# Weighing values by whole fp32 products on the two column halves of TensorE

## The chip, the core and the metric

One core of one Trainium2 chip runs the program. TensorE (PE in the profile, PEld its weight loads) multiplies, VectorE (DVE) and ScalarE (ACT) do the elementwise work, GpSimd (POOL) small work, and SyncE (SP) issues most of the transfers. The metric is the device time of one execution in microseconds; the kernel before took 608.46 us (median of 3 runs, 608.0 to 609.45).

## The reference, cut to what matters

Two layers of an encoder on 256 tokens of width 1024, all in fp32. Each layer is an attention sublayer with 16 heads of width 64 in three groups, each head with its own 256 x 256 matrix of probabilities, and then a gated feed-forward sublayer of width 2816.

```python
def mixer_sublayer(x, n1, w_in_l, qg, kg, rpb_l, og, w_out_l, tables):
    h = rms_norm(x, n1)
    proj = h @ w_in_l
    ...
    out_a = neighbourhood_attention(qa, ka, heads(va, H_NA), ...)   # 4 heads
    out_d = dilated_window_attention(qd, kd, heads(vd, H_DIL), ...) # 6 heads
    out_c = gqa_block_attention(qc, kc, heads(vc, H_GKV))           # 6 heads, 2 sets of keys and values
    mix = jnp.concatenate([rms_norm(out_a, ...), rms_norm(out_d, ...), rms_norm(out_c, ...)], axis=-1)
    return x + mix @ w_out_l

def channel_sublayer(x, n2, w_gu, cw, cb, w_dn):
    g, u = jnp.split(rms_norm(x, n2) @ w_gu, 2, axis=-1)
    g = depthwise_conv_centred(g, cw, cb)
    return x + (jax.nn.gelu(g, approximate=False) * u) @ w_dn
```

What the change touches is, in every head, the last step: p = softmax(scores), then p times the head's values (256 x 256 by 256 x 64).

## The kernel before, in words

**Split parts.** The kernel gets fp32 accuracy out of products of the type fp32r: each operand is split into a large part (`hi`, the cast) and a little part (`lo`, what the cast leaves), and `mm3` (L708) makes one product of three: large by large, large by little, little by large. ACT makes the large parts and DVE the little ones, for the weights (`split`, L676, tiles `wp_hi` and `wp_lo`) as for the activations. The profile's names follow the buffers: `psw_w` and `psa_a` are the two pools of PSUM banks.

**Attention.** In each layer the projections run first as a "filler" on TensorE, between them and then between the output projections the steps of the heads are woven in (`Weave`, L764; the loop at L1298). A head's steps are `scores` (L1226: products of 64 rows, two heads side by side on the two row halves of TensorE, kept together in bursts by `nc.together()`), `softens` (softmax on DVE and ACT), `turn` (L1105) and `weigh` (L1121, called by L1261). `turn` transposes the probabilities with four TensorE transposes into one PSUM tile, which ACT copies as the large part (`act_ch`) and from which DVE makes the little part (`act_cl`). `weigh` multiplies values by the turned probabilities: for each of two blocks of 128 keys, three products of a 128 x 128 stationary operand and 256 moving columns. The stationary operand is a head's 64 columns of values beside 64 columns of zeros (`beside_zeros`, L1065; tiles `const_v`, whose zeros GpSimd writes at the start, L601), on the left for an even head and on the right for an odd one, so that both heads of a pair add into one PSUM tile of 128 rows. So a pair takes 12 products, and a layer has 8 pairs. `mixed` (L1130) reads the sum into the operands of the output projection.

**The order of the work** is not the program's order. `Plan` (L239) records all instructions first. `order` (L323) then simulates the engines with the costs of `cost` (L475) and takes, again and again, the instruction that could start first; among equals the lowest rank goes first. The rank is the instruction's number in the program, shifted by `later` and by the table `PLACES` (L229), which holds a shift for single instructions by number. The start of matmuls on PE is reckoned by `run_on_pe` (L385). The first 13 loads (`START`, L45: the input, the identity, gains and the first four chunks of weights, on SP's and ACT's queues) are given fixed landing times by their place in the program (`LANDS`, L52, used at L450), wherever the order puts them. Each engine then runs its instructions strictly in the order that comes out.

The kernel fills the first microseconds of PE with products of no use (`warmed`, L581; `const_warm`).

Of the kernel before, what the change touches and what calls it, by code (L numbers as in the profile page):

```python
# [36 lines left out]
UNIT = 2048  # L37
BANK = 512
NS2K = 5


RAWS, PARTS, AHEAD, CHUNK = 4, 2, 2, 512
# [182 lines left out]
def handover(a, b):  # L225
# [1 line left out]


PLACES = {  # L229
# [6 lines left out]
}  # L236


class Plan:  # L239
# [83 lines left out]
    def order(self):  # L323
# [60 lines left out]

        def run_on_pe(o, at):  # L385

            half = o.kind == "half"
            if pe is None:
                return at + 109, o.ns, half, False
            start, ns, was, open_ = pe  # L390
            if half and was:
                ld = max(start + 3, at)
                if open_:
                    return max(start + 4, ld + (0 if at <= start + 3 else 109)), o.ns, half, False
                return max(start + 113, ld + 109), o.ns, half, True
            if half or was:
                return max(start + ns + 92, at) + 108, o.ns, half, True
            return max(start + ns, max(start + 3, at) + (106 if o.kind == "turn" else 110)), o.ns, half, False

        done = []  # L400
        gone = [False] * len(ops)
# [1 line left out]
        while len(done) < len(ops):  # L403
# [71 lines left out]
def cost(engine, method, args, kw, ins):  # L475
# [42 lines left out]
def encoder_kernel(  # L518
# [70 lines left out]
    with nc.later(1000):  # L589
# [299 lines left out]
    for l in range(DEPTH):  # L889
# [161 lines left out]
                transposed(pairs(zs[t], first, n), both, t, f"{what}{group}{l}{t}")  # L1051
            return both

        def values(places, src, t):

            hi, lo = places
            r = rx[:, t : t + 1]
# [3 lines left out]
        def values_of(tiles, ps, c0, t, nh):  # L1061
            src = ps[:, c0 : c0 + nh * HD].rearrange("p (h d) -> p h d", d=HD)
            values([z[:, t, 1 : 2 * nh : 2] for z in tiles], src, t)

        def beside_zeros(tiles, h, odd):  # L1065

            i = 2 * h + 1 - odd
            return [z[:, :, i : i + 2].rearrange("p t m d -> p t (m d)") for z in tiles]


        class Head:
# [33 lines left out]
            def turn(self):  # L1105
                name = self.name
                tp = psw.tile([P, NT, S], F32, tag="w", name=f"tp_{name}")
                for kt in range(NT):
                    for t in range(NT):
                        nc.tensor.transpose(  # L1110
                            tp[:, kt, t * P : (t + 1) * P], self.p[:, t, kt * P : (kt + 1) * P], ident
                        )
                self.pT = [
                    act.tile([P, NT, S], F32R, tag=g, name=f"pT{g}_{name}", bufs=2) for g in ("ch", "cl")
                ]
                hi, lo = self.pT
# [4 lines left out]
            def weigh(self, op, first, last):  # L1121

                hi, lo = self.pT
                for kt in range(NT):
                    mm3(
                        op, self.v[0][:, kt], self.v[1][:, kt], hi[:, kt], lo[:, kt],
                        first and kt == 0, last and kt == NT - 1,
                    )

        def mixed(op, gi, i):  # L1130

# [113 lines left out]

        heads = []
        for h in range(H_DIL):
            heads.append(Head("d", h, h, [dil[:, t] for t in range(NT)], beside_zeros(vown, h, h % 2)))
        for h in range(H_GQ):
            kv = h // (H_GQ // H_GKV)  # L1250
            heads.append(Head("c", h, kv, None, beside_zeros(vkv, kv, h % 2)))
        for h in range(H_NA):
            heads.append(Head("a", h, h, na_bias(h), beside_zeros(vown, h, h % 2)))

        def values_a():
            for t in range(NT):
# [2 lines left out]
        groups = [(gi, h) for gi, n in enumerate((H_DIL, H_GQ, H_NA)) for h in range(n)]  # L1259

        def weigh(i):  # L1261
            gi, h = groups[i]
            if h % 2 == 0:
                hold["op"] = psw.tile([P, S], F32, tag="w", name=f"o_{l}{i}")
            heads[i].weigh(hold["op"], h % 2 == 0, h % 2 == 1)
            if h % 2 == 1:
                with nc.later(MIX_LATER):
                    mixed(hold["op"], gi, h // 2)

        prep_d("q", gq)  # L1270
        wv.until("dk")
# [26 lines left out]
        for i in range(len(heads) + 2):  # L1298
            for part in range(3):
                if (i, part) in hooks:  # L1300
                    with nc.later(PREP_LATER):
                        hooks[i, part]()
                if part == 0 and i < len(heads) and i % 2 == 0:
                    scores(i)
                elif part == 1 and 0 <= i - 1 < len(heads):
                    heads[i - 1].turn()
                elif part == 2 and 0 <= i - 2 < len(heads):
                    weigh(i - 2)
                    if i - 2 in (7, 12):
                        group_rstd((i - 2) // 12)  # L1310
        wv.fill(1e9)
        group_rstd(2)

# [238 lines left out]
```

## Time and profile before

| | before |
|---|---|
| median of 3 runs | 608.46 us |
| lowest, highest | 608.0, 609.45 us |
| span of the profiled execution, first to last instruction | 606.6 us |
| PE busy in it | 600.9 us (99%) |
| DVE busy | 484.9 us (80%) |
| ACT busy | 428.6 us (71%) |
| POOL busy | 80.9 us (13%) |

The span is what the trace shows of one execution; the profiled execution has no other time of its own in the data, and the median of the runs lies 1.8 us above its span. A line of the timeline gives the start in us from the start of the span, the length in us of one or several instructions merged, the engine, the operation with out<-in and shapes, and how many. The lengths of neighbouring matmuls overlap: what one costs in a row of them is the distance from start to start. All instructions carry line L472, the one place that emits them, so they are told apart by tile names. The notes on waits in brackets give the idle time before an instruction and what ended it.

### The profile page before, as it was taken

The numbers are of one execution on the slowest core, as the hardware profiler recorded it, in microseconds if no ns is written. First come the engines' busy times: TensorE is split into PE (matmuls) and PEld (weight loads), VectorE is DVE, ScalarE is ACT, GpSimd is POOL, SyncE is SP. The second block draws the span as 40 slices with busy tenths as digits, with TensorE's granted clock in tenths as the row PEclk, the third lists the DMA queues.
The fourth block names the chain that finished last, engine by engine and source line by source line (L and its number), as shares of the span: only waits on it lengthen the run. The fifth ranks groups of instructions, "written<-read, shape, count | busy, mean of one in ns | idle before, by whom it ended". The sixth has DMA issues, their size and how long they took to land.

```text
span 606.6 us, 9899 instructions
## 1 busy us (share of the span) xinstructions
PE 600.9 (99%) x3496; PEld 526.7 (87%) x3496; DVE 484.9 (80%) x995; ACT 428.6 (71%) x1065; POOL 80.9 (13%) x130
## 2 busy tenths in 40 slices
PE   8999999999999999999999999999999999999997
PEld 7999898888888888888899989888888888888886
DVE  4899897997788988887777898777977777777775
ACT  6889999686666767666688899676765555665661
POOL 2733030103400000000022214421000000000000
PEclk9999999999999999999999999999999999999999
DMA  8994303566598899988455726844465555555601
GB/s 280 296 294 140 105 36 107 195 202 228 185 224 297 278 342 322 318 304 290 153 147 162 248 70 243 291 163 139 142 205 209 174 175 206 184 166 207 199 9 69
DMA packets 85217, 121.44 MB, mean 200 GB/s; under 512 B 9880, under 2 KB 69880, under 8 KB 85168
## 3 DMA queue, kind: packets, MB, share of 16 engines
q1 hardware_dynamic: 82896, 112.17, 56.3%
q0 software_dynamic: 1728, 8.39, 3.9%
q8 instruction: 27, 0.44, 0.3%
q10 hardware_dynamic: 544, 0.26, 0.2%
q14 instruction: 22, 0.18, 0.1%
HBM read 110.93 MB, written 9.88 MB: 199 GB/s over the span
## 4 chain that ended last, share of the span: by engine, by line
PE 96%; ACT 2%; DVE 1%; POOL 0%; issue 0%; DVEq 0%; ACTq 0%; POOLq 0%
PE psw_w L472 53%; PE psa_a L472 43%; ACT act_s2k L472 1%; ACT wp_hi L472 0%; DVE act_z L472 0%; DVE wp_lo L472 0%; POOL small_rstd L472 0%; ACT act_z L472 0%; ACT act_hT L472 0%; DVE act_sw L472 0%; POOL small_ms L472 0%; DVE const_x L472 0%; DVE act_qo L472 0%; POOL const_warm L472 0%; DVEq L472 0%
## 5 line engine op out<-in xcount | busy, mean ns | idle before, releaser
L472 DVE TENSOR_TENSOR wp_lo<-wp_raw,wp_hi 128x512 fp32r<-128x512 f32 (+2 forms) x332 | 231.5, 731 | 59.1 <-ACT wp_hi L472 39.3
L472 ACT CAST wp_hi<-wp_raw 128x512 fp32r<-128x512 f32 (+2 forms) x332 | 203.0, 663 | 22.8 <-PE psw_w L472 10.2
L472 PE MATMUL psw_w<-act_hT,wp_hi 128*128 128x512 f32 x704 | 180.4, 393 | 0.0
L472 PEld LDWEIGHTS psw_w<-act_hT,wp_hi 128*128 128x128 f32 x704 | 127.8, 189 | 24.8 <-DVE act_hT L472 0.7
L472 PE MATMUL psa_a<-wp_hi,act_hT 128*128 128x384 f32 (+2 forms) x448 | 113.1, 333 | 0.7 <-ACT wp_hi L472 0.7
L472 PEld LDWEIGHTS psw_w<-act_hT,wp_lo 128*128 128x128 f32 x704 | 97.7, 190 | 6.8
L472 PE MATMUL psw_w<-act_hT,wp_lo 128*128 128x256 f32 x704 | 102.2, 282 | 0.0
L472 PEld LDWEIGHTS psa_a<-wp_hi,act_hT 128*128 128x128 f32 x448 | 78.3, 189 | 3.4 <-ACT wp_hi L472 0.9
L472 ACT COPY act_s2k<-psw_w 128x256 f32<-128x256 f32 x88 | 32.4, 373 | 62.2 <-PE psw_w L472 61.9
L472 PE MATMUL psa_a<-wp_lo,act_hT 128*128 128x384 f32 (+2 forms) x224 | 74.4, 334 | 0.1
L472 PE MATMUL psa_a<-wp_lo,act_ch 128*128 128x512 f32 (+1 forms) x176 | 68.9, 392 | 0.0
L472 PE MATMUL psa_a<-wp_hi,act_ch 128*128 128x512 f32 x176 | 68.8, 392 | 0.0
L472 PE MATMUL psa_a<-wp_hi,act_cl 128*128 128x512 f32 (+1 forms) x176 | 68.5, 393 | 0.0
L472 DVE TENSOR_TENSOR act_s2k<-psw_w,act_s2k 128x256 f32<-128x256 f32 x88 | 36.6, 421 | 14.5 <-ACT act_s2k L472 14.1
L472 PEld LDWEIGHTS psa_a<-wp_lo,act_hT 128*128 128x128 f32 x224 | 42.2, 189 | 2.4 <-DVE wp_lo L472 1.0
L472 PEld LDWEIGHTS psa_a<-wp_hi,act_cl 128*128 128x128 f32 x176 | 33.1, 188 | 7.5
L472 PEld LDWEIGHTS psa_a<-wp_hi,act_ch 128*128 128x128 f32 x176 | 33.2, 189 | 6.7
L472 PEld LDWEIGHTS psa_a<-wp_lo,act_ch 128*128 128x128 f32 x176 | 33.1, 188 | 6.7
L472 DVE SCALAR_TENSOR_TENSOR act_s2k<-act_s2k,act_cw,act_s2k 128x255 f32<-128x255 f32 x88 | 36.7, 477 | 1.4 <-ACT act_s2k L472 1.3
L472 ACT ACTIVATE act_s2k<-act_s2k 128x512 f32<-128x512 f32 x22 | 13.9, 631 | 30.2 <-DVE act_s2k L472 30.2
L472 ACT ACTIVATE act_s2k<-act_s2k,act_cw 128x256 f32<-128x256 f32 x44 | 24.1, 595 | 15.3 <-DVE act_s2k L472 15.3
L472 POOL TENSOR_TENSOR small_rstd<-small_ms,const_mh 128x6 f32<-128x6 f32 (+2 forms) x26 | 30.8, 1186 | 14.4 <-DVE small_ms L472 12.8
(132 smaller groups left out, 791.6 us busy)
## 6 DMA issues: line engine op xcount, KB each, us to landing
wp_raw<-in_w_gate_up_dram SPq DMA_DIRECT2D x44, 1024.0 KB, 5.1
wp_raw<-in_w_down_dram SPq DMA_DIRECT2D x22, 1024.0 KB, 7.3
wp_raw<-in_w_in_dram SPq DMA_DIRECT2D x14, 768.0 KB, 6.0
wp_raw<-in_w_in_dram SPq DMA_DIRECT2D x8, 1024.0 KB, 9.1
wp_raw<-in_w_out_dram SPq DMA_DIRECT2D x8, 768.0 KB, 8.4
dram_khi<-act_mixT_hi SPq DMA_DIRECT2D x4, 768.0 KB, 3.6
dram_klo<-act_mixT_lo SPq DMA_DIRECT2D x4, 768.0 KB, 8.3
wp_lo<-dram_klo POOLq DMA_DIRECT2D x4, 768.0 KB, 4.8
```

Source lines behind the costliest of these rows:

```text
L472: getattr(o.engine.real, o.method)(*map(real, o.args), **{k: real(v) for k, v in o.kw.items()})
```

## The change

The probabilities and the values are no longer split. ACT copies the turned probabilities once, as fp32, into one of six buffers `pT`; values are written once as fp32, without zeros beside them; DVE's subtractions for both go, and GpSimd's zeroing of the values' tiles. A pair's weighing becomes four products on whole fp32 operands: for each of two blocks of keys, one product per head with 64 stationary columns, the even head writing rows 0 to 63 and the odd head rows 64 to 127 of the PSUM tile, all four kept together as a burst. The planner gets a kind of matmul, "side", for these: 216 ns from start to start, and its result counted 379 ns after those 216, where other matmuls have 163. `PLACES` is a new table, and now has entries for the first loads too.

```diff
+NPT = 6
+
+TURN_ACT = ("dca", "dca")
+WEIGHED = {1: 1, 3: 1, 5: 1, 7: 1, 9: 1, 11: 1, 13: 1, 15: 1}
+AFTER = {7: 0, 12: 1}
...
 PLACES = {
-    375: -35, 488: 15, 528: -53, 550: 173, 587: -78, 594: 125, 616: -286, 646: -9, 709: -79, 750: -226, 752: -396,
...
+    37: -45, 39: -9, 63: 39, 65: -40, 79: 98, 82: -21, 85: -21, 95: -172, 107: 206, 109: -238, 110: -222, 120: 24,
...
-            half = o.kind == "half"
+            mode = o.kind if o.kind in ("half", "side") else None
...
-            if half and was:
+            if mode == "side" and was == mode:
+                return max(start + ns, max(start + 3, at) + 109), o.ns, mode, True
+            if mode and mode == was:
                 ld = max(start + 3, at)
...
-            if half or was:
-                return max(start + ns + 92, at) + 108, o.ns, half, True
+            if mode or was:
+                return max(start + ns + 92, at) + 108, o.ns, mode, True
...
-                end = pe[0] + o.ns + (218 if o.kind == "turn" else 163)
+                end = pe[0] + o.ns + {"turn": 218, "side": 379}.get(o.kind, 163)
...
+        if args[1].width() < P:
+            return 216.0, 0, 0, "side"
...
     vown, vkv = (
-        [const.tile([P, NT, 2 * n + 1, HD], F32R, tag=f"v{n}{i}", name=f"v{n}{i}") for i in range(2)]
-        for n in (H_DIL, H_GKV)
+        const.tile([P, NT, n, HD], F32, tag=f"v{n}", name=f"v{n}") for n in (H_DIL, H_GKV)
     )
-    for z in vown + vkv:
-        nc.gpsimd.memset(z[:, :, 0::2].bitcast(F32), 0.0)
...
-            nc.scalar.activation(hi, src, AF.Copy, scale=r)
-            nc.vector.scalar_tensor_tensor(lo, src, r, hi.bitcast(F32), ALU.mult, ALU.subtract)
...
+            nc.scalar.activation(z[:, t, :nh], src, AF.Copy, scale=rx[:, t : t + 1])
...
+                self.pT = act.tile([P, NT, S], F32, tag="pT", name=f"pT_{name}", bufs=NPT)
                 with nc.later(TURN_LATER):
-                    nc.scalar.copy(hi, tp)
-                    nc.vector.tensor_tensor(lo, tp, hi.bitcast(F32), op=ALU.subtract)
...
+                    if name[0] in TURN_ACT[odd]:
+                        nc.scalar.copy(self.pT, tp)
+                    else:
+                        nc.vector.tensor_copy(self.pT, tp)
...
         def weigh(i):
-            gi, h = groups[i]
-            if h % 2 == 0:
-                hold["op"] = psw.tile([P, S], F32, tag="w", name=f"o_{l}{i}")
-            heads[i].weigh(hold["op"], h % 2 == 0, h % 2 == 1)
...
+            if i not in WEIGHED:
+                return
+            ends = range(i - 2 * WEIGHED[i] + 2, i + 1, 2)
+            ops = [psw.tile([P, S], F32, tag="w", name=f"o_{l}{j}") for j in ends]
+            with nc.together():
+                for j, op in zip(ends, ops):
+                    for kt in range(NT):
+                        for z, rows_ in zip(heads[j - 1 : j + 1], (LOW, HIGH)):
+                            nc.tensor.matmul(op[rows_], z.v[:, kt], z.pT[:, kt], start=kt == 0, stop=kt == NT - 1)
+            with nc.later(MIX_LATER):
+                for j, op in zip(ends, ops):
+                    gi, h = groups[j]
+                    mixed(op, gi, h // 2)
```

Counted from the start of the new program, number 37 is the load of the third chunk of weights and number 39 that of input chunks 4 and 5, the eighth and tenth entries of `START`; the four writes of zeros ahead of them are gone.

More of the change, by code (lines that the diff above doesn't have):

```diff
@@ L1052, in by_pairs, with values_of @@
             return both
-        def values(places, src, t):
-            hi, lo = places
-            r = rx[:, t : t + 1]
-            nc.scalar.activation(hi, src, AF.Copy, scale=r)
-            nc.vector.scalar_tensor_tensor(lo, src, r, hi.bitcast(F32), ALU.mult, ALU.subtract)
-        def values_of(tiles, ps, c0, t, nh):
+        def values_of(z, ps, c0, t, nh):
             src = ps[:, c0 : c0 + nh * HD].rearrange("p (h d) -> p h d", d=HD)
[L1063 to L1068, printed above, removed]
+            nc.scalar.activation(z[:, t, :nh], src, AF.Copy, scale=rx[:, t : t + 1])
         class Head:
@@ L1112, in turn @@
                         )
[L1113 to L1116, printed above, removed]
+                odd = self.h % 2
+                self.pT = act.tile([P, NT, S], F32, tag="pT", name=f"pT_{name}", bufs=NPT)
                 with nc.later(TURN_LATER):
-                    nc.scalar.copy(hi, tp)
-                    nc.vector.tensor_tensor(lo, tp, hi.bitcast(F32), op=ALU.subtract)
[L1121 to L1128, printed above, removed]
+                    if name[0] in TURN_ACT[odd]:
+                        nc.scalar.copy(self.pT, tp)
+                    else:
+                        nc.vector.tensor_copy(self.pT, tp)
         def mixed(op, gi, i):
@@ L1247, in encoder_kernel @@
         for h in range(H_DIL):
-            heads.append(Head("d", h, h, [dil[:, t] for t in range(NT)], beside_zeros(vown, h, h % 2)))
+            heads.append(Head("d", h, h, [dil[:, t] for t in range(NT)], vown[:, :, h]))
         for h in range(H_GQ):
             kv = h // (H_GQ // H_GKV)
-            heads.append(Head("c", h, kv, None, beside_zeros(vkv, kv, h % 2)))
+            heads.append(Head("c", h, kv, None, vkv[:, :, kv]))
         for h in range(H_NA):
-            heads.append(Head("a", h, h, na_bias(h), beside_zeros(vown, h, h % 2)))
+            heads.append(Head("a", h, h, na_bias(h), vown[:, :, h]))
         def values_a():
@@ L1308, in encoder_kernel @@
                     weigh(i - 2)
-                    if i - 2 in (7, 12):
-                        group_rstd((i - 2) // 12)
+                    if i - 2 in AFTER:
+                        group_rstd(AFTER[i - 2])
         wv.fill(1e9)
```

11 lines of the change are left out of this document (4 added, 7 removed), and 24 rows, old and new, of the table PLACES.

## The prediction

> **What bounds the kernel now.** First the page: busy time by engine, and the chain that ended last.
>
> ```profile
> PE 600.9 (99%) x3496; PEld 526.7 (87%) x3496; DVE 484.9 (80%) x995; ACT 428.6 (71%) x1065; POOL 80.9 (13%) x130
> ...
> GB/s 280 296 294 140 105 36 107 195 202 228 185 224 297 278 342 322 318 304 290 153 147 162 248 70 243 291 163 139 142 205 209 174 175 206 184 166 207 199 9 69
> ...
> PE 96%; ACT 2%; DVE 1%; POOL 0%; issue 0%; DVEq 0%; ACTq 0%; POOLq 0%
> ```
>
> PE carries 96% of the chain. An average hides stages, so the second view is the busy time in the two stretches where heads are weighed, one in each layer:
>
> ```profile
> 57.00:110.00 53.00, 53.00 (x379) 46.68 (x379) 46.55 (x125) 49.78 (x140) 10.47 (x15) 1.00 0.26 85
> 354.00:410.00 56.00, 56.00 (x400) 49.48 (x399) 45.40 (x121) 46.49 (x134) 18.03 (x27) 1.00 0.60 208
> ```
>
> The columns are length, then PE, PEld, DVE, ACT and POOL. PE is busy for all 53.00 of 53.00 and 56.00 of 56.00 us. Busy matmuls overlap, so the third view is the timeline of PE, where start to start gives the price of one:
>
> ```profile
> 106.73 0.40 PE L472 MATMUL psw_w<-act_ch,const_v 128*128 128x256 f32 x2
> 106.97 0.28 PE L472 MATMUL psw_w<-act_cl,const_v 128*128 128x256 f32 x1
> 107.08 0.40 PE L472 MATMUL psw_w<-act_ch,const_v 128*128 128x256 f32 x2
> 107.32 0.28 PE L472 MATMUL psw_w<-act_cl,const_v 128*128 128x256 f32 x1
> 107.43 0.40 PE L472 MATMUL psw_w<-act_ch,const_v 128*128 128x256 f32 x2
> 107.67 0.28 PE L472 MATMUL psw_w<-act_cl,const_v 128*128 128x256 f32 x1
> 107.79 0.28 PE L472 MATMUL psw_w<-act_ch,const_v 128*128 128x256 f32 x1
> 107.91 0.39 PE L472 MATMUL psa_a<-wp_lo,act_mixT_hi 128*128 128x512 f32 x1
> ...
> 112.10 0.39 PE L472 MATMUL psa_a<-wp_lo,act_mixT_hi 128*128 128x512 f32 x1
> 112.33 0.39 PE L472 MATMUL psa_a<-wp_hi,act_mixT_lo 128*128 128x512 f32 x1
> ```
>
> Ten weighing products lie between 106.73 and 107.91, 0.118 us each, with no hole; a product of 512 columns takes 0.23 (112.10 to 112.33). So each 256 further columns cost 0.112. PE is the bound, packed to its issue distance: the change is worth what it does to PE's stream, plus what the new order does to PE's few stalls.
>
> **The change part by part.** *Weighing products removed.* Their count:
>
> ```profile
> L472 PE MATMUL psw_w<-act_ch,const_v 128*128 128x256 f32 x128 | 27.9, 285 | 0.0
> L472 PE MATMUL psw_w<-act_cl,const_v 128*128 128x256 f32 x64 | 18.4, 287 | 0.0
> ```
>
> 128 + 64 = 192 products, 12 for each of 16 pairs of heads. A pair takes 12 x 0.118 = 1.42 us of PE, all pairs 22.7 us.
>
> *Whole products added.* A pair now takes 4 products of 256 columns. No matmul of whole fp32 operands that isn't a transpose is in the trace, so its price is bounded. A whole product gives what three split ones give (large by large, large by little, little by large), and little by little besides: as three passes over 256 columns it costs 0.118 + 2 x 0.112 = 0.34 us, as four 0.118 + 3 x 0.112 = 0.45. I take four, since nothing lets an array that only takes the parts leave one out. The Trainium skill's page "FP8 and Floating Point Precision", section "TensorE Precision Notes", says four passes for true FP32; no run here shows it yet.
>
> Whether the two heads of a pair run side by side decides most. The nearest rows are those of the scores, two heads on two row halves:
>
> ```profile
> 45.04 0.33 PE L472 MATMUL psa_a<-wp_lo,act_hT 128*128 128x384 f32 x1
> 45.22 0.34 PE L472 MATMUL psa_a<-wp_hi,act_hT 128*128 128x384 f32 x1
> 45.48 1.70 PE L472 MATMUL psw_w<-act_ko,act_qo 64*128 64x256 f32 x24
> 47.11 0.50 PE L472 MATMUL psa_a<-wp_hi,act_hT 128*128 128x256 f32 x2
> ...
> 47.57 0.40 PE L472 MATMUL psa_a<-wp_hi,act_hT 128*128 128x256 f32 x2
> ```
>
> The full product at 45.22 has streamed by 45.39 (0.17 each). The two products after the burst take 0.50 where two normally take 0.40, so they really begin at 47.21. Between lie 1.82 us for 24 half products: one by one they would need 24 x 0.118 = 2.83, in pairs 12 x 0.118 = 1.42. So pairs run together, and 0.40 us is lost on going into the burst and out of it. I carry both over to column halves, since a burst of half arrays between full ones is what both are. The Trainium skill's "TensorEngine Tiling", section "Key Properties", has the rule that speaks against this change: a change of tiling mode drains TensorE. The trace agrees, with 0.40 us for one burst; without this toll the sum would be 16 x 0.40 = 6.4 us lower.
>
> A burst then costs 0.40 + 2 x 0.454 = 1.31 us against 1.42: 0.11 less, and over 16 bursts **1.7 us less**. The ends: three passes give 0.40 + 0.68 = 1.08, or 5.4 us less; the planner's own 216 ns a product in the diff (864 for four) gives 1.26, or 2.4 less.
>
> *DVE, ACT, GpSimd.* The subtractions go from DVE, one copy per head stays on ACT:
>
> ```profile
> L472 DVE TENSOR_TENSOR act_cl<-psw_w,act_ch 128x512 fp32r<-128x512 f32 x32 | 21.9, 684 | 4.5 <-ACT act_ch L472 4.4
> ...
> L472 ACT CAST act_ch<-psw_w 128x512 fp32r<-128x512 f32 x32 | 18.9, 593 | 5.6 <-PE psw_w L472 5.4
> ```
>
> That is 32 x 0.684 = 21.9 us of DVE. It earns nothing by itself: DVE is covered by PE in both stretches (46.55 of 53.00). ACT is the next engine (49.78 of 53.00), and its work for the turned probabilities stays. If PE's part of that stretch shrinks by 8 x 0.11 = 0.9 us, ACT still has 2.3 us to spare, so no new bound. A head's operand is ready 0.68 us earlier, as nothing waits for DVE. On the other side a burst now needs both heads before its first product, and all of PE's queue behind it waits if the second head's copy is late. Before, the even head's six products could go earlier. Other products stand between turning and weighing, and the 0.68 more than pays; I cost it at nothing, and if that cover is gone at 0.59 (the copy) for a pair that stalls. The zeroing on GpSimd at the start has nobody waiting for it: nothing.
>
> *The new list: first loads.* Loads 37 (third chunk of weights) and 39 (input chunks 4 and 5) get shifts of -45 and -9: ranks -8 and 30, below 31 of the first gains. All loads of SP can start at once for the planner, so rank decides, and both go to the head of SP's queue, ahead of gains, identity and the first two chunks of weights. The planner sees no cost in this: landing times go by place in the program. Before:
>
> ```profile
> 0.73 0.39 SPq L472 DMA_DIRECT2D act_s2k<-in_norm_g_dram  x1
> 1.18 0.41 SPq L472 DMA_DIRECT2D const_ident<-in_c_ident_dram  x1
> 1.63 0.91 SPq L472 DMA_DIRECT2D wp_raw<-in_w_in_dram  x2
> ...
> 5.66 0.51 ACT L472 CAST wp_hi<-wp_raw 128x384 fp32r<-128x384 f32 x1 [2.64 <-DMA wp_raw<-in_w_in_dram]
> 6.77 0.48 ACT L472 ACTIVATE act_hT<-psw_w,const_gains 128x256 fp32r<-128x256 f32 x1 [0.60 <-DVE wp_lo L472]
> ...
> 14.16 0.61 PE L472 MATMUL psa_a<-wp_hi,act_hT 128*128 128x384 f32 x2 [0.69 <-ACT wp_hi L472]
> ...
> wp_raw<-in_w_in_dram SPq DMA_DIRECT2D x4, 192.0 KB, 4.2
> const_x<-in_x_dram SPq DMA_DIRECT2D x3, 256.0 KB, 4.3
> ```
>
> ACT waits for the first chunk until 5.66, and PE still waits for ACT at 14.16: the start hangs on ACT, which hangs on the first loads. 192 + 256 = 448 KB ahead of them at the first slice's 280 GB/s is 1.6 us. ACT's idle 0.60 at 6.77 would take up a part. I put **1.0 us** on it; the ends are 0 (ACT is given other work first) and 1.6.
>
> *The new list: the rest.* It is made for the new costs, and what it can still win is PE's stalls:
>
> ```profile
> PEld psa_a L472 <- DVE wp_lo L472: 1.0, 3, 0.4
> ...
> PEld psa_a L472 <- ACT wp_hi L472: 0.9, 1, 0.9
> ```
>
> About 2 us in all, 0.9 of it the stall at 14.16. With DVE relieved I take **0.6 us less**, from 1.5 less to 1.0 more (190 moved instructions can also open new stalls).
>
> Sum: -1.7 + 1.0 - 0.6 = -1.3 us. The profiled span of 606.6 becomes 605.3; the median of the runs lies 1.8 above it, so 608.5 becomes **607.2 us**.
>
> **The rivals.** *B, the halves out of step: slower.* The scores run at one 0.118 a pair, so there both halves start together. If a whole product is two instructions of half its length, issued head by head in order, the odd head starts its first when the even head starts its second. Each burst then ends half a product (0.23 us) later, and the drain waits for it. The burst costs 1.31 + 0.23 = 1.54, 0.12 more than now; over 16, 1.9 more, and with +1.0 - 0.6 the time is 610.8. It decides against the change once a burst costs over 1.42. For it: the planner counts the side product's result 379 ns after its 216, where others have 163, just 216 more, as if a second half of 216 followed. Against it: the planner lets the next full product start after 216 + 92 + 108. The Trainium skill's "TensorE: Matmul & The Clock Gate", section "The mechanism", says that matmuls start and end in program order, which by itself puts no step between halves.
>
> *C, the loads eat it.* With the full 1.6 at the start and no gain elsewhere: -1.7 + 1.6 = -0.1, 608.4 us.
>
> *D, the halves don't run together.* Then the change doesn't do what it says: 4 x 0.454 + 0.40 = 2.22 a burst, 0.80 more, 12.8 over 16: 621 us. Against it stand the 24 score products in 1.82 us, but those share no rows.
>
> *E, three passes:* 5.4 less + 0.4 = 603.5.
>
> **How the numbers follow.** About 0.2% (1.2 us) is what a measurement of this kernel can tell from no change. Chances: the forecast 0.50 (its own range 605.0 to 608.8, of it 0.36 faster, 0.13 same, 0.01 slower); B 0.27 (0.07 same, 0.20 slower); C 0.12 (0.09 same, the rest even); D 0.06, slower; E 0.05, faster. Faster 0.43, same 0.29, slower 0.28. The range, 604.5 to 611.2, takes in the forecast, C and most of B; D, E and the ends of B are left out.
>
> **What would show it.** In the timeline after: bursts of side products with 1.3 us from the last full product's end to the next one's start (1.5 says B, 2.2 says D); no `act_cl<-psw_w` on DVE; ACT's first cast at about 6.7 to 7.2 and PE's full stream about 1 us later than at 14.16; both weighing stretches still without PE idle. New waits of PE for the `pT` copies, or of PE's loads for `wp_lo` in the feed-forward stage, would make the prediction wrong.

## The result, and the profile after

The changed kernel takes 612.48 us (median of 4 runs, 612.33 to 612.54); the kernel before took 608.34 beside it on the same chip. The ratio is 1.0065 (95% interval 1.005 to 1.0079): slower by 4.0 us, where 1.3 us faster had been forecast. The profiled execution spans 610.6 us, against 606.6.

Busy time by engine and the chain that ended last, from the page of the kernel after:

```profile
PE 599.4 (98%) x3432; PEld 510.0 (84%) x3432; DVE 462.9 (76%) x951; ACT 426.1 (70%) x1065; POOL 83.1 (14%) x126
...
PE 87%; ACT 3%; issue 3%; POOL 3%; DVE 2%; DMA 2%; SPq 0%; ACTq 0%; POOLq 0%; DVEq 0%
```

PE has 64 matmuls fewer and is busy 1.5 us less, DVE 22 us less: the subtractions are gone. Yet PE carries only 87% of the chain, where it carried 96%: what was lost is not work but waiting. What PE waited for, in us in total, times, and the longest one:

```profile
PE psa_a L493 <- DVE wp_lo L493: 3.5, 2, 2.3
PE psw_w L493 <- DMA const_ident<-in_c_ident_dram: 1.5, 1, 1.5
PE psw_w L493 <- ACT act_s2k L493: 1.1, 1, 1.1
```

None of these three stood in the view before, which had two:

```profile
PE psw_w L472 <- POOL const_warm L472: 1.0, 1, 1.0
PE psa_a L472 <- ACT wp_hi L472: 0.7, 1, 0.7
```

First the part that went well, on PE's timeline:

```profile
106.05 0.40 PE L493 MATMUL psa_a<-wp_lo,act_mixT_hi 128*128 128x512 f32 x1
106.38 1.08 PE L493 MATMUL psw_w<-act_pT,const_v 128*64 128x256 f32 x8
107.39 0.50 PE L493 MATMUL psa_a<-wp_hi,act_mixT_lo 128*128 128x512 f32 x1
107.73 0.39 PE L493 MATMUL psa_a<-wp_hi,act_mixT_hi 128*128 128x512 f32 x1
```

The full product at 106.05 has streamed by 106.28 (0.23 each). The one behind the burst takes 0.50 where one normally takes 0.39, so it really begins at 107.50. A burst of a pair therefore costs 1.22 us. All 16 of them come to between 1.16 and 1.22, 19.0 us in all by the records, against 1.42 and 22.7 before: PE's stream became 3.2 to 3.7 us shorter, twice what was forecast. Then the stalls. At the start, 1.5 us for the identity, which is now issued at 2.13 behind three other loads:

```profile
0.73 0.38 SPq L493 DMA_DIRECT2D wp_raw<-in_w_in_dram  x1
1.17 0.42 SPq L493 DMA_DIRECT2D const_x<-in_x_dram  x1
1.63 0.46 SPq L493 DMA_DIRECT2D act_s2k<-in_norm_g_dram  x1
2.13 0.42 SPq L493 DMA_DIRECT2D const_ident<-in_c_ident_dram  x1
...
5.65 0.20 PE L493 MATMUL psw_w<-const_ident,act_s2k 16*128 16x16 f32 x1 [1.52 <-DMA const_ident<-in_c_ident_dram]
...
6.05 0.51 ACT L493 CAST wp_hi<-wp_raw 128x384 fp32r<-128x384 f32 x1 [3.03 <-DMA wp_raw<-in_w_in_dram]
```

At 25 us, DVE's split of a weight chunk takes 2.21 instead of its usual 0.55, beside a copy of GpSimd for the bias table, and PE waits for it:

```profile
22.90 1.83 POOL L493 COPY act_nab<-act_few 28x1984 f32<-28x1984 f32 x1
22.94 2.21 DVE L493 TENSOR_TENSOR wp_lo<-wp_raw,wp_hi 128x384 fp32r<-128x384 f32 x1
...
25.20 0.45 PE L493 MATMUL psa_a<-wp_lo,act_hT 128*128 128x384 f32 x1 [1.22 <-DVE wp_lo L493]
25.80 0.55 DVE L493 TENSOR_TENSOR wp_lo<-wp_raw,wp_hi 128x384 fp32r<-128x384 f32 x1
```

The kernel before has the same copy, and there too it meets a step of DVE: two small steps that otherwise take 0.32 together take 1.96. But PE does not wait for those; the new order has put a weight split in their place.

```profile
24.12 2.16 POOL L472 COPY act_nab<-act_few 28x1984 f32<-28x1984 f32 x1
24.51 1.96 DVE L472 TENSOR_TENSOR act_sw<-act_z,act_sdq 128x48 f32<-128x48 f32 x2
```

At 45 us, the new order has put the bias table's mask on DVE ahead of four such splits. The mask waits 3.17 us for the gathers of the table (`act_nab<-dram_scr`), issued from 33.28 on, and all that stands behind it on DVE waits too, and then PE:

```profile
33.28 3.09 SPq L493 DMA_DIRECT2D act_nab<-dram_scr  x2
...
43.99 0.76 DVE L493 SCALAR_TENSOR_TENSOR act_nab<-act_nab,const_na 128x576 f32<-128x576 f32 x1 [3.17 <-DMA act_nab<-dram_scr]
...
45.13 2.09 DVE L493 TENSOR_TENSOR wp_lo<-wp_raw,wp_hi 128x384 fp32r<-128x384 f32 x4
...
45.73 0.44 PE L493 MATMUL psa_a<-wp_lo,act_hT 128*128 128x384 f32 x1 [2.26 <-DVE wp_lo L493]
```

Before, the gathers are issued from 30.11 on, and the three masks run without a wait:

```profile
40.88 2.08 DVE L472 SCALAR_TENSOR_TENSOR act_nab<-act_nab,const_na 128x576 f32<-128x576 f32 x3
```

In the weighing stretches, busy time of PE, PEld, DVE, ACT and POOL:

```profile
57.00:110.00 53.00, 51.94 (x349) 40.05 (x348) 40.27 (x120) 50.60 (x147) 10.09 (x13) 1.00 0.26 86
354.00:410.00 56.00, 55.80 (x386) 44.02 (x386) 36.67 (x114) 49.55 (x146) 17.31 (x26) 1.00 0.60 208
```

DVE has 6 and 9 us less there. PE has holes for the first time, and ACT is busy for 50.60 of 53.00.

To weigh stalls against products, I take from the matmul records the distance between the ends of two neighbours, less what is usual for that form, and add up all that is over 0.3 us. Before this gives 1.3 us (two places), after 8.7 (eight places). Bursts 3.4 shorter (the middle of 3.2 and 3.7) and stalls 7.4 longer make +4.0, which is the difference of the spans. The same sum serves for the experiments.

### The profile page after: what moved, and what is told of

It reads as the page before. It is cut to its first block, busy times and chain, and to the rows that moved or that the text cites. A ratio compares the mean times of both kernels' runs of the same rounds, so it can differ in the third digit from the quotient of the medians.

```text
span 610.6 us, 9692 instructions
## 1 busy us (share of the span) xinstructions
PE 599.4 (98%) x3432; PEld 510.0 (84%) x3432; DVE 462.9 (76%) x951; ACT 426.1 (70%) x1065; POOL 83.1 (14%) x126
## 4 chain that ended last, share of the span: by engine, by line
PE 87%; ACT 3%; issue 3%; POOL 3%; DVE 2%; DMA 2%; SPq 0%; ACTq 0%; POOLq 0%; DVEq 0%
PE psw_w L493 50%; PE psa_a L493 37%; ACT act_s2k L493 2%; POOL small_rstd L493 2%; DMA wp_raw<-in_w_in_dram 1%; ACT wp_hi L493 1%; DVE wp_lo L493 1%; DMA const_x<-in_x_dram 1%; DVE act_z L493 0%; POOL small_ms L493 0%; ACT act_hT L493 0%; POOL act_sck L493 0%; DVE const_x L493 0%; SPq L493 0%; DVE act_sw L493 0%
## 5 line engine op out<-in xcount | busy, mean ns | idle before, releaser
L493 DVE TENSOR_TENSOR wp_lo<-wp_raw,wp_hi 128x512 fp32r<-128x512 f32 (+2 forms) x332 | 236.5, 742 | 47.0 <-ACT wp_hi L493 32.4
L493 PE MATMUL psa_a<-wp_hi,act_ch 128*128 128x512 f32 (+1 forms) x176 | 67.1, 393 | 0.0
L493 POOL TENSOR_TENSOR small_rstd<-small_ms,const_mh 128x6 f32<-128x6 f32 (+2 forms) x26 | 32.7, 1257 | 17.5 <-DVE small_ms L493 15.8
L493 ACT ACTIVATE act_s2k<-act_s2k,small_rs 128x256 f32<-128x256 f32 x64 | 29.4, 516 | 0.2 <-DVE small_rs L493 0.2
```

The costliest lines, as they stand in the source:

```text
L493: getattr(o.engine.real, o.method)(*map(real, o.args), **{k: real(v) for k, v in o.kw.items()})
```

## The experiments

Two theories stood at the beginning. **L, the list:** the products save some 3 us, and the new order of the list loses about 7, part of it with the first loads. **P, the products:** the new products and their bursts are themselves what costs, through holes and waits around them. Later a third question came up: which engine binds once PE has less to do. Times are medians. The ratio is to the kernel before on the same chip. Stalls are the sum just described.

| kernel | us | ratio (95%) | span | PE's stalls |
|---|---|---|---|---|
| before | 608.34 to 608.92 by chip | 1 | 606.6 | 1.3 |
| after | 612.48 | 1.0065 (1.005 to 1.0079) | 610.6 | 8.7 |
| first loads back | 609.84 | 1.002 (1.0012 to 1.0029) | 608.4 | 5.7 |
| no list | 609.12 | 1.0012 (1.0003 to 1.0021) | 607.2 | 4.5 |
| before, no list | 612.72 | 1.007 (1.0057 to 1.0083) | 610.3 | 5.0 |
| order of before | 607.74 | 0.9989 (0.9979 to 0.9998) | 605.8 | 4.2 |
| before, first loads moved | 611.17 | 1.0041 (1.0027 to 1.0055) | 609.4 | 3.5 |
| table later | 609.48 | 1.0009 (1.0 to 1.0017) | 607.9 | 5.0 |
| masks later alone | 611.0 | 1.0033 (1.0019 to 1.0047) | 610.3 | 6.3 |
| copy in pieces | 613.27 | 1.0079 (1.0064 to 1.0094) | 610.7 | 7.6 |
| odd copies on DVE, no list | 607.12 | 0.9975 (0.9965 to 0.9985) | 605.1 | 3.2 |
| odd copies on DVE, order of before | 610.51 | 1.0029 (1.0019 to 1.0039) | 608.7 | 6.8 |
| odd copies on DVE, new list | 612.13 | 1.0057 (1.0042 to 1.0073) | 610.5 | 8.2 |
| odd copies on DVE, table later | 613.86 | 1.0092 (1.0079 to 1.0106) | 611.9 | 9.3 |
| two pairs a burst | 610.0 | 1.0017 (1.0007 to 1.0027) | 608.2 | 5.2 |
| halves in turn | 607.85 (one run) | | 606.1 | 4.4 |
| heads apart | 621.58 (one run) | | 619.8 | 1.7 |

**The new list without its first loads.**

```
-    37: -45, 39: -9, 63: 39, 65: -40, 79: 98, 82: -21, 85: -21, 95: -172, 107: 206, 109: -238, 110: -222, 120: 24,
+    63: 39, 65: -40, 79: 98, 82: -21, 85: -21, 95: -172, 107: 206, 109: -238, 110: -222, 120: 24,
```

> The changed kernel, with the two entries of the new list taken out that moved the third chunk of weights and input chunks 4 and 5 to the head of SP's queue; all else as changed. Theory L (the products save about 3 us, the new list loses about 7, part of it at the start): the wait of PE for the identity (1.5 us) goes, ACT's first cast comes at about 5.7 again, 612.5 becomes 611.0 to 611.5. Theory P (the products and their bursts make the loss, the list is neutral): at the start the same change, but the time moves by less than 0.5 us, as the start's delay is taken up again before the weighing.

It gave back 2.6 us of the 4.0, more than either theory expected: two of 204 entries cost more than the whole gain that had been forecast. Not all of it need be the loads: the planner works the order out anew, and by the records some 60 matmuls of the first 48 us stand at other places.

**The same two shifts in the kernel before** tell whether that cost is the loads' own; here only some ten matmuls change places.

```
-    375: -35, 488: 15, 528: -53, 550: 173, 587: -78, 594: 125, 616: -286, 646: -9, 709: -79, 750: -226, 752: -396,
+    41: -45, 43: -9, 375: -35, 488: 15, 528: -53, 550: 173, 587: -78, 594: 125, 616: -286, 646: -9, 709: -79, 750: -226, 752: -396,
```

> The kernel before, old products and old list, with only the two first loads moved ahead as in the change (numbers 41 and 43 there). Theory L (the first loads delay everything behind them by what PE waits for the identity, 1.5 us, and push later transfers): 608.5 becomes 610.0 to 611.2, the same 1.5 to 2.7 us that taking them back gave the changed kernel. Rival (the delay only costs where the new list leaves no room): under 1 us, 608.5 to 609.5.

2.5 us more by the ratio (the medians, 608.92 and 611.17, lie 2.25 apart), the same as above within the intervals. The start of this kernel shows where most of it begins:

```profile
2.13 0.42 SPq L472 DMA_DIRECT2D const_ident<-in_c_ident_dram  x1
...
5.66 0.26 PE L472 MATMUL psw_w<-const_ident,act_s2k 16*128 16x16 f32 x1 [1.50 <-DMA const_ident<-in_c_ident_dram]
5.89 0.51 ACT L472 CAST wp_hi<-wp_raw 128x384 fp32r<-128x384 f32 x1 [2.87 <-DMA wp_raw<-in_w_in_dram]
...
8.16 1.44 PE L472 MATMUL psw_w<-const_warm 128*128 128x256 bf16 x6
```

The identity is issued at 2.13 instead of 1.18, and PE, which needs it for its first transpose, waits 1.50 for it. ACT's first cast starts only 0.2 us later than before. The last six products of no use ahead of the real work then take 1.44, where before they take 0.82:

```profile
6.57 0.82 PE L472 MATMUL psw_w<-const_warm 128*128 128x256 bf16 x6
```

So PE's first product of the projections starts at 9.30 instead of 7.30. At 18 us PE is 1.25 us behind by the records, as the wait of 0.69 for ACT at 14.16 is gone, and from 55 us on 2.5. In four of the five profiled executions with the first loads moved, these six take 1.44 to 1.49. In that of the kernel after they take 0.82, in spite of its wait of 1.52, and in all those with the loads at their old places 0.82 to 0.97. What decides it stays open.

**No list at all,** for the new products and for the kernel before.

```
-PLACES = {
...
-}
+PLACES = {}
```

> The changed kernel with an empty list of shifts: the planner's own greedy order for the new products. Theory L: the three large stalls of PE (1.2 us at 25, 2.3 us at 45, 1.1 us at 58) belong to places where the list put single instructions, so most of them go and the time falls below 612.5, to about 609 to 611. Theory P: the stalls stay in some form, 612 or more.

> The kernel before with an empty list of shifts: the planner's own greedy order for the old products. It shows what a list is worth: Theory L, for which lists matter by several us, expects 609.5 to 612. Theory P expects 608 to 609.5. The difference to the changed kernel without list is the products' worth in greedy orders: about 3 us faster with the new products by L, none or slower by P.

Between these two the products differ, and with them the planner's own order: 612.72 to 609.12, 3.6 us less (the first of these lies 0.7 above what L had expected), about what the bursts give (3.2 to 3.7), with stalls alike (5.0 and 4.5). Theory P falls. The whole way from before to after can now be walked in measured steps: dropping the old list costs 4.2 (608.53 to 612.72), the new products give 3.6 (to 609.12), and the new list costs 3.4 (to 612.48, on another chip, where before took 608.34). The new list was worse than none; without its first loads (609.84) it was no better than none, where the old one had been worth 4.2.

**The new products in the order of before,** forced by a list of places, with a pair's burst where its last product stood.

```
+FORCED = [0, 30, 31, 1, 29, 2, 32, 33, 3, 4, 34, 5,
...
-            best = None
-            for e, r in ready.items():
+            i = FORCED[len(done)]
+            best = (max(ops[i].at, idle_at(ops[i].engine.name)), 0, i)
+            for e, r in ():
```

> The new products in the order of the kernel before: every instruction that both kernels have stands in the old order on its engine, removed ones are left out, and the four products of a pair stand together where the last of its twelve stood. Theory L: 16 bursts of 1.22 us instead of 1.42 and no new stalls: 608.4 becomes 605.0 to 605.8. Theory P: bursts that need both heads and drain the array make PE wait wherever they stand: 608.5 or more.

A miss: 607.74, 0.8 us less than before and not some 3. The bursts are nearly as short as in the kernel after (1.16 to 1.27 us), but 2.9 us came back as stalls:

```profile
PE psw_w L497 <- POOL act_sqm L497: 0.7, 2, 0.4
...
PE psw_w L497 <- DVE act_z L497: 0.7, 1, 0.7
PE psw_w L497 <- ACT act_s2k L497: 0.5, 2, 0.3
```

PE comes to each transpose earlier, and the engines that make its operands do not. In this order they were just in time for the longer bursts.

**The bias table later.** The list without its first loads, with the copy, the gathers and the masks of the first layer's table moved behind the places at which they held DVE.

```
 order of the list without its first loads, by numbers of instructions in the program, but
+the copy of GpSimd (304) behind 490
+the store and the two gathers (305, 412, 413) behind 799
+the three masks (701, 702, 703) behind 1112
```

> The changed kernel with the first loads back, in its own order, except that the seven instructions that make the table of the neighbourhood heads' bias in layer 0 (GpSimd's copy, its store and the two gathers on SP's queue, the three masks on DVE) stand later: the copy behind the third group's statistics, the transfers behind the load of weight unit 13, the masks behind the load of unit 15. Theory L (PE's stalls at 25 to 45 us come from DVE held by GpSimd's copy, 1.6 us, and by the mask that waits for the gathers, 1.1 us): both go, 609.8 becomes 607.0 to 608.0. Rival (they come from the first casts and loads themselves): the stalls stay at the same places, 609.3 to 610.

A miss: 609.48, about 0.7 us less by the ratios (1.002 to 1.0009), where two to three had been expected, and the intervals overlap. The stalls at those places went, and PE waited a little further on:

```profile
PE psw_w L497 <- ACT act_s2k L497: 1.3, 2, 1.1
...
PE psw_w L497 <- DVE act_z L497: 0.7, 2, 0.5
```

**The masks alone, in the changed kernel's own order.**

```
 order of the kernel after, but
+the three masks (701, 702, 703) behind 1112
```

> The changed kernel with its own order, but the three masks of the bias table stand on DVE behind the next stretch of weight loads, so that DVE does not wait for the gathers ahead of wp_lo. If that wait makes the stall of 2.26 us at 45.7 and nothing is late right behind it: 610.2 to 610.8. If something else comes due at the same time (ACT's casts, DVE's lateness from the stall at 25.2), half of it or more stays: 611.4 to 612.5.

611.0 us: by the ratios 1.9 us less than after (1.0065 to 1.0033, with intervals that just part), between the two expectations. The 2.26 at 45.7 went and so did the 1.06 for `act_s2k`, while 0.7 for `act_z` and 0.3 for `act_s2k` came. The wait for the gathers is a true part of the loss.

**GpSimd's copy in four pieces,** in the changed kernel's own order.

```
-        nc.gpsimd.tensor_copy(
-            rows_.rearrange("p (n c) -> p n c", c=RPB_C),
-            nabs["few"].unsqueeze(1).to_broadcast([NR, GRID_W, RPB_C]),
-        )
+        for n0 in range(0, GRID_W, 16):
+            nc.gpsimd.tensor_copy(
+                rows_[:, n0 * RPB_C : (n0 + 16) * RPB_C].rearrange("p (n c) -> p n c", c=RPB_C),
+                nabs["few"].unsqueeze(1).to_broadcast([NR, 16, RPB_C]),
+            )
```

> The changed kernel with its own order, and GpSimd's copy of 28 x 1984 cut into four of 28 x 496 at the same place. If DVE is held until the end of the copy that it meets, the step of 2.21 us becomes about 1.0 or less, and the stall of 1.22 us at 25.2 falls below 0.4: 611.3 to 612. If GpSimd's copying slows DVE as long as it lasts, or the wait is not GpSimd's, the stall stays: 612.3 to 613.

613.27 us, no better than after. The timeline shows what becomes of the copy and of DVE:

```profile
24.32 3.21 POOL L497 COPY act_nab<-act_few 28x496 f32<-28x496 f32 x4
24.36 0.98 DVE L497 TENSOR_TENSOR wp_lo<-wp_raw,wp_hi 128x384 fp32r<-128x384 f32 x1
...
26.13 0.95 DVE L497 TENSOR_TENSOR wp_lo<-wp_raw,wp_hi 128x384 fp32r<-128x384 f32 x1
```

The two engines take turns: each DVE step now meets one piece and takes 0.95 to 0.98 instead of 0.55, and the four pieces need 3.21 us instead of 1.83. DVE is late by about as much, in small portions. PE's wait here does fall, from 1.22 to 0.58, and that at 45 us from 2.26 to 1.42. Why the time doesn't is not shown. In the profiled execution the last six products of no use take 1.49, as in the kernel before with the first loads moved, and PE's projections start at 9.57 instead of 7.73. That execution ends only 0.1 us later than the one of after, so the pieces may have won what the start lost. The Trainium skill's page "SBUF — State Buffer", section "Who interferes with whom", has the rule: a DVE instruction with two inputs in SBUF contends with a GpSimd instruction that reads SBUF, since the two engines share ports there, and one locks the other out. The trace agrees: 2.21 us for a step of 0.55 that starts 0.04 behind the start of a copy of 1.83 and ends 0.42 behind its end.

**The odd heads' copies on DVE,** with no list, to see whether ACT binds.

```
-TURN_ACT = ("dca", "dca")
+TURN_ACT = ("dca", "")
```

> The new products without a list, and the turned probabilities of odd heads copied by DVE, not by ACT. If ACT has become what PE waits for in the weighing stretches once PE's part is shorter (ACT busy 50 of 53 us there): 609.1 becomes 606.5 to 608. If the waits there are the order's alone: 608.8 to 609.8.

607.12 us: 2.2 less than with all copies on ACT by the ratios (1.0012 to 0.9975), and the fastest version of all, 0.25% below the kernel before. The load did change hands. In the stretches, with the copies on ACT:

```profile
57.00:110.00 53.00, 52.33 (x347) 38.99 (x347) 38.87 (x107) 49.36 (x140) 10.72 (x15) 1.00 0.29 92
354.00:410.00 56.00, 54.66 (x366) 41.55 (x365) 35.91 (x103) 46.81 (x135) 17.85 (x27) 1.00 0.60 208
```

and with the odd ones on DVE:

```profile
57.00:110.00 53.00, 52.46 (x351) 39.75 (x350) 44.24 (x118) 45.73 (x131) 12.12 (x15) 1.00 0.31 101
354.00:410.00 56.00, 55.96 (x373) 42.76 (x372) 40.83 (x114) 44.19 (x128) 18.31 (x27) 1.00 0.60 209
```

ACT falls from 49.36 to 45.73 in the first stretch, where its load was highest, and PE gains 0.13 there. PE gains its 1.30 in the second. That is another wait, which the order with all copies on ACT has and this one has not:

```profile
PE psa_a L472 <- DMA wp_hi<-dram_khi: 1.3, 1, 1.3
```

It is for a weight part that had been stored and is read back through GpSimd's queue. By the records it is 1.6 of the stalls of 4.5; without it 2.9 would be left, and 3.2 are left with the copies on DVE. So the time expected came, and not for the reason: ACT's load earned nothing that shows.

**The same edit in three other orders:** that of before, that of the new list, and that of the list with the table later.

> The new products in the order of before (607.74 with all copies on ACT), and the odd heads' copies of the turned probabilities on DVE. If ACT's load is what was left of the loss there (waits of PE for act_s2k and, through ACT, for act_sqm), about 1.2 to 2 us go: 605.7 to 606.5. If it is DVE and GpSimd that PE waits for (act_z 0.67, act_sqm 0.72), more work on DVE brings nothing or makes those waits longer: 607.5 to 609.

> The changed kernel with its own list, the odd heads' copies on DVE. If ACT's load makes the whole loss, the time falls as it did without a list, by 2.3 us and more: 609.5 to 610.3 or less. If the first loads, the GpSimd copy that holds a DVE step and the mask ahead of its gathers make it, as the stalls of 1.5, 1.2 and 2.3 us say, those stay, only the 1.06 us wait for act_s2k goes, and the time is 611 to 612.5.

> The new list without its first loads, with the bias table later (609.48), and the odd heads' copies on DVE. There PE waited 1.3 us for ACT's act_s2k and 0.7 for DVE's act_z. If ACT is the next limit that the list meets: 1.3 to 2.2 us less, 607.3 to 608.2. If the list itself is what costs (its order of the steps, whichever engine runs them): 609 to 610.

None of the three shows ACT's load to bind. In the order of before the edit costs 2.4 us by the ratios (0.9989 to 1.0029), more than either expectation had:

```profile
PE psa_a L497 <- DMA wp_hi<-dram_khi: 1.3, 1, 1.3
PE psw_w L497 <- DVE act_z L497: 1.1, 1, 1.1
```

Here the wait for the part read back comes up, 1.5 us by the records, and DVE's `act_z` is later than with the copies on ACT (1.1 against 0.7). With the new list nothing much changes (612.13). With the table later it costs 5 us (1.0009 to 1.0092), far outside both expectations, as PE waits for copies on DVE and for what is queued behind them:

```profile
PE psw_w L497 <- DVE act_pT L497: 2.0, 2, 1.9
PE psw_w L497 <- ACT act_z L497: 1.6, 2, 0.9
```

The same edit thus gives from 2.2 us less to 5 us more, by which steps happen to be late in the order around it.

**Two pairs a burst,** with no list, to pay the way into a burst and out of it less often.

```
-WEIGHED = {1: 1, 3: 1, 5: 1, 7: 1, 9: 1, 11: 1, 13: 1, 15: 1}
+WEIGHED = {3: 2, 5: 1, 9: 2, 11: 1, 15: 2}
```

> The new products without a list, and two pairs of heads weighed in one burst where a group allows it: 10 bursts in place of 16. By the toll of 0.35 us for going into a burst and out of it, 6 x 0.35 = 2.1 us less: 609.1 becomes 607.0. If the longer wait for four heads opens new stalls of PE, as the rival theory P would have it: 609 or more.

No gain: 610.0. A joint burst costs 2.03 to 2.08 us by the records, against 2 x 1.21, so the six save the 2.1 us expected. One wait takes as much, and it is not one for four heads. It stands in a burst of a single pair, heads 10 and 11 of the first layer: the even head's first product runs, and the other six records wait for ACT's copy of the second head, which stands behind softmax steps on ACT.

```profile
100.81 0.65 PE L472 MATMUL psw_w<-act_pT,const_v 128*64 128x256 f32 x2
103.53 1.24 PE L472 MATMUL psw_w<-act_pT,const_v 128*64 128x256 f32 x6 [2.08 <-ACT act_pT L472]
```

Behind this wait the granted clock of TensorE, the third column from the end in the next view, is 0.57 for 4 us. It is 1.00 in the 4 us before and behind.

```profile
104.00:108.00 4.00, 4.00 (x15) 2.92 (x13) 1.81 (x3) 3.46 (x8) 0.73 (x1) 0.57 0.00 0
```

That is about 1.7 us more (an estimate, 0.43 x 4). Why it came here is not shown: behind the stall of 2.26 us in the kernel after, the granted clock stays at 1.00 (46 to 52 us). So this run does not say whether joint bursts pay.

**The halves in turn:** the order of before, and in a burst both steps of the even head first.

```
-                    for kt in range(NT):
-                        for z, rows_ in zip(heads[j - 1 : j + 1], (LOW, HIGH)):
+                    for z, rows_ in zip(heads[j - 1 : j + 1], (LOW, HIGH)):
+                        for kt in range(NT):
```

> The new products in the order of before, but a pair's four steps of the even head come first and the four of the odd head behind them, so that two steps in a row always use the same half of the columns. If two products on different halves run at the same time (the burst of 1.22 us holds 0.864 of steps), a burst now holds 8 steps of 0.216 one after another: 1.73 + 0.35 = 2.08 us, 0.86 more at each of 16 places, so about 607.7 + 13.8 = 621.5. If the halves take turns in any case and a step is simply short, the order costs nothing: 607 to 608.5.

607.85, and the burst is as long as it was:

```profile
100.71 1.09 PE L497 MATMUL psw_w<-act_pT,const_v 128*64 128x256 f32 x8
```

Taken alone this can mean two things: the halves run side by side whatever the order, or a product takes half as long as I thought and the halves run one behind the other. The next kernel parts them.

**Heads apart:** the order of before, and each head weighed by itself at the place of its last product, with full-width work between.

```
-            with nc.together():
-                for j, op in zip(ends, ops):
-                    for kt in range(NT):
-                        for z, rows_ in zip(heads[j - 1 : j + 1], (LOW, HIGH)):
-                            nc.tensor.matmul(op[rows_], z.v[:, kt], z.pT[:, kt], start=kt == 0, stop=kt == NT - 1)
+            if h % 2 == 0:
+                hold["op"] = psw.tile([P, S], F32, tag="w", name=f"o_{l}{i + 1}")
+            op, z, rows_ = hold["op"], heads[i], (LOW, HIGH)[h % 2]
+            for kt in range(NT):
+                nc.tensor.matmul(op[rows_], z.v[:, kt], z.pT[:, kt], start=kt == 0, stop=kt == NT - 1)
```

> The new products in the order of before, each head weighed by itself as soon as its copy is there: two whole products of one half of the columns, then full-width work, then the two of the other half. If a whole product takes two steps of 0.216 (four passes) and the halves run side by side in a burst of a pair, a burst of one head holds 4 steps, 0.86, and 0.36 of toll, 1.22, as long as a pair's: 1.22 more at each of 16 pairs, 607.7 + 19.5 = about 627. If the two records of a product run side by side and a product takes one step of 0.216, whichever half it uses, a burst of one head is 0.43 + 0.36 = 0.79, and a pair costs one more toll: 0.36 x 16 = 5.8 more, about 613.5.

621.58 us. The burst of one head:

```profile
106.42 0.39 PE L497 MATMUL psa_a<-wp_hi,act_mixT_lo 128*128 128x512 f32 x1
106.73 1.08 PE L497 MATMUL psw_w<-act_pT,const_v 128*64 128x256 f32 x4
107.74 0.50 PE L497 MATMUL psa_a<-wp_hi,act_mixT_hi 128*128 128x512 f32 x1
```

Four records take the 1.08 that eight took, and from 106.65 to 107.85 the burst costs 1.20: one head is as dear as two. So a whole product is two records of 0.216 in a row, and the two halves run side by side. The time is less than the 627 expected by this theory since two of the pairs came together again (30 bursts and not 32) and PE's stalls fell from 4.2 to 1.7: bursts 16.6 us longer in all, stalls 2.5 shorter, 14.1 together, against 14.0 between the spans. The stalls are the second message: with PE slower again, the waits that the quick bursts had laid open are gone.

## Why the prediction was wrong, point by point

*What bounds the kernel: right for before.* PE did carry it, and a shorter stream was worth something: 3.6 us between the two kernels without a list.

*Weighing, -1.7: right in kind, too small in size.* Four passes held: 0.432 a product, where I had put 0.454. The halves side by side held (heads apart), so rivals B and D fall; E, three passes, falls by the 0.432. For four passes the Trainium skill's page "FP8 and Floating Point Precision", section "TensorE Precision Notes", agrees with the trace. The toll of a burst was 0.35 (1.22 less 0.864) or less, not the 0.40 of the scores. That makes -3.2 to -3.7. The drain on a change of tiling mode, which the Trainium skill's "TensorEngine Tiling (Array Packing)", section "Key Properties", states, was paid at every burst, if the toll of 0.30 to 0.36 is that drain, and did not decide.

*The second head's stall, nothing: right for this change.* No wait of PE for `act_pT` stands in the view after. It appeared at 2.1 us in the kernel with two pairs a burst, in a burst of one pair: the case that I had costed at 0.59 if it came.

*"ACT still has 2.3 us to spare, so no new bound": half right.* No engine became the bound, ACT's load the least: relieving it by 3.6 us gave PE 0.13 in that stretch. But I concluded from it that the shorter bursts are kept. A margin that is an average over 53 us says nothing of the single handover: PE came to some operands of ACT, DVE and GpSimd before they were there, and in the old order this took 2.9 of the 3.4 us.

*First loads, +1.0: too small, and the wrong chain.* They cost 2.5 and 2.6 us in two kernels. I followed ACT's first cast, which I put at 6.7 to 7.2 and which came at 6.05. What was late was the identity, 0.95 later in SP's queue, for which PE waited 1.5 us, and in the kernel before the same shifts came with slower products of no use behind it (1.44 against 0.82). I had quoted its row as one of those that are overtaken and not asked who waits for it. Rival C, that the loads eat the gain, had them too cheap as well (1.6), and it is not the whole: without them the kernel still takes 609.84.

*The rest of the list, -0.6: the step that failed.* I held that the list "is made for the new costs, and what it can still win is PE's stalls", with at most 1.0 more. In the terms of my sum, the products gave -3.4 and the first loads +2.6 of the +4.0, so that +4.8 is left for this term, where I had put -0.6. Some 2.9 of it are the stalls that the shorter bursts meet in the order of before already; the other 1.9 is what the list without its first loads costs against that order (ratios 0.9989 and 1.002). It opened stalls of 1.2, 2.3 and 1.1 us besides the first one, and it replaced a list that had been worth 4.2 us. I had seen that the planner misses the cost of the first loads and did not draw the conclusion for the rest: a list that was found by a model is only as good as the model, and leans on what the model leaves out. Here that was the wait for the gathers and the turns that DVE and GpSimd take. That the list leans on them is an inference; that each place costs is measured for the first loads (2.5) and the masks (about 1.9), and not separable for GpSimd's copy.

*What would show it.* New waits of PE's loads for `wp_lo` I had named as a sign of error, but in the feed-forward stage; they came at 25 and 45 us. The weighing stretches were not without idle PE.

What stays open: single repairs of the new list do not add up (first loads 2.6, then the table only 0.7 more); in the traces, PE runs on from a place that is cleared to the next one that is late. I did not find an order that keeps the whole 3.4 us.

## What to carry to other kernels

Where the engine that binds has its work packed without holes, a cheaper operation is worth its saving only as far as the engines that feed it can come earlier too: look at the margin at each handover, not over the stretch. Measure a new operation and a new order apart, the operation with the same plain order on both sides; here 3.6 us won and 7.6 lost stood behind a total of 4.0 lost. And when loads change places at the start, ask of every load that is overtaken, small ones above all, who waits for it.

## What the runs showed of the hardware

Two products on different halves of TensorE's columns run side by side even where all steps of the one stand ahead of all steps of the other: with the halves in turn the burst of eight records took 1.09 us, as in the other order, while four records of one half alone took 1.08. By the records, they start in pairs some 13 ns apart, where those of one half alone start 0.216 us apart or more, so a pair is one of each half. The rule that I had leant on against rival B (the Trainium skill's "TensorE: Matmul & The Clock Gate", section "The mechanism": matmuls start and end in program order) does not hold for these. A DVE step with two inputs in SBUF that starts just behind a GpSimd copy is held until about the copy's end (2.21 instead of 0.55 us; it ends 0.42 behind the copy), and cutting the copy makes both take turns (3.21 instead of 1.83 us for the copy).
